# Tokens on the output's partitions for two FFNs and all down and output projections

## The chip, the core and the metric

The kernel runs on one core of a Trainium2 chip. TensorE multiplies matrices out of SBUF into the eight banks of PSUM; VectorE (DVE), ScalarE (ACT) and GpSimd (POOL) work on tiles of 128 partitions; SyncE (SP) issues the DMAs that load the weights. Each engine takes its instructions in the program's order and waits on semaphores for the others. The metric is the time of one execution on the device in microseconds (us), the median of several runs.

## The reference

256 tokens of width 2048 go through a first block twice and through a second block once. A layer of the first block:

```python
h = rmsnorm(x, g_pre_mix[l])
proj = h @ w_in[l]                                     # 2048 x 4608
y_a = conformer_conv(proj[..., :a_end], ...)           # width 512
y_b = dilated_attention(proj[..., a_end:b_end], ...)   # width 1024, 16 heads
y_c = pool_mixer(proj[..., b_end:], ...)               # width 512
y = concatenate([rms_normalize(y_a), rms_normalize(y_b), rms_normalize(y_c)]) * g_mix[l]
x = x + rmsnorm(y @ w_out[l], g_post_mix[l])           # 2048 x 2048
h = rmsnorm(x, g_pre_ffn[l])
f = (silu(h @ w_gate[l]) * (h @ w_up[l])) @ w_down[l]  # 2048 x 5632, twice; 5632 x 2048
x = x + rmsnorm(f, g_post_ffn[l])
```

The second block has the same frame: four branches of width 512 (a gated delta rule, a linear recurrent unit, spatial gating, a short convolution), an output projection of 2048 x 2048, and an FFN with a causal convolution over the tokens behind gate and up. All is float32. The output is compared in float32, which sets how the products are made (below).

## The kernel before

All activations lie with features on the partitions and the 256 tokens along the free axis: a tile of 128 features is [128, 256], the residual x is [128, 16, 256]. Both factors of a product are split into two parts, hi and lo, of TensorE's faster float32 type, and three products (hi hi, hi lo, lo hi) stand for one.

Weights come as a stream (class `Stream`): half chunks of 256 rows by 512 columns, 512 KB each, 1120 in all, in the order of a plan that lists them chunk by chunk. For each, SP issues a load into `st` (4 buffers), ScalarE makes `whi` (L87, 5 buffers) and VectorE `wlo` (L95, 4 buffers). `ahead(i)` emits the splits three half chunks before the products that use them.

`groupA` makes 512 columns of output, features on the output's partitions: for each half chunk four tiles of 128 columns, two row tiles k and three products, 24 matmuls of a stationary weight tile [128, 128] against a moving activation [128, 256] (`mms`, L340 to L342). `dualA` runs the first two groups of a half block together, while the residual is still being updated (`barrier`). Its `step(n)` emits `prep(i)`, which adds f times its norm to x and makes the split operand `hhi`, `hlo` for two row tiles. `groupB` is used for the attention's values and one input of the spatial gating only: the activation [128, 128 tokens] is stationary, the weights [128, 512] move, and 12 matmuls make [128 tokens, 512] in each of two banks (L396 to L398).

The order of the work around the products is made by the program itself. After each half chunk's matmuls `pump()` emits what stands in queues of generators: evacuations of PSUM (`evq`), and background work (`bg`, `hot`), each with an estimate of its VectorE time; the budget is 1450 ns a half chunk, and `yield -1` rests until the next half chunk.

A norm is applied after the products. `R_gen` sums squares on TensorE (`ps_st`), makes the reciprocal root on GpSimd (`rsqrt`, twelve small steps), broadcasts it over the partitions by TensorE (`bcast`, `ps_bc`) and copies it to SBUF as R and Rh; the evacuations multiply by it. An FFN (`ffn`, `ffn_run`) goes over 11 pieces j of 512 hidden columns, gate then up, in three portions, with the down products of a portion behind it; its evacuations make `hid`, the split operand of the down products. f [128, 16, 256] gathers the down or output products. In the last column groups (`last_group`) each part of f gets its squares summed (`sq_add`) and its gain (`gains`); for the very last one `fin_last` takes tile by tile, and `post` (`rsqrt_fast`) makes the norm that `barrier` multiplies by. There are six such ends: three mixers and three FFNs. A mixer's output projection runs by branch: yC, yA (8 half chunks each), then the attention's yb (16), with the attention in the background of the first two.

## Time and profile before

| | before |
|---|---|
| median of 3 runs | 3460.69 us (3459.11 to 3462.64) |
| span of the profiled execution | 3458.9 us |
| TensorE busy, matmul records | 3423.8 us (99%), 27758 |
| VectorE busy | 2180.8 us (63%) |
| ScalarE busy | 1648.5 us (48%) |
| GpSimd busy | 105.0 us (3%) |
| mean granted TensorE clock | 0.993 of full speed |
| read from HBM | 598.84 MB, 175 GB/s over the span |

The profile shows one execution. What lies around its span isn't recorded apart: the runs' median is 1.8 us above it. A matmul's record overlaps the next one's, so the pace of a stream is read from the starts of its records, or from their count in a stretch, not from the length of one. PE is TensorE's matmuls, PEld its weight loads.

### The profile page before, as it was taken

The numbers are of one execution on the slowest core, as the hardware profiler recorded it, in microseconds if no ns is written. First come the engines' busy times: TensorE is split into PE (matmuls) and PEld (weight loads), VectorE is DVE, ScalarE is ACT, GpSimd is POOL, SyncE is SP. The second block draws the span as 40 slices with busy tenths as digits, with TensorE's granted clock in tenths as the row PEclk, the third lists the DMA queues.
The fourth block names the chain that finished last, engine by engine and source line by source line (L and its number), as shares of the span: only waits on it lengthen the run. The fifth ranks groups of instructions, "written<-read, shape, count | busy, mean of one in ns | idle before, by whom it ended". The sixth has DMA issues, their size and how long they took to land.

```text
span 3458.9 us, 66199 instructions
## 1 busy us (share of the span) xinstructions
PE 3423.8 (99%) x27758; PEld 3365.6 (97%) x27758; DVE 2180.8 (63%) x2957; ACT 1648.5 (48%) x2219; POOL 105.0 (3%) x301
## 2 busy tenths in 40 slices
PE   9999999999999999999999999999999999999999
PEld 9989999999999998999999999999999999999998
DVE  6877755455555787775545555578665766466465
ACT  5556544444344555554444334455435554455344
POOL 0000000000000000000000000001110000000000
PEclk9999999999999999999999999999999999999999
DMA  7654566666665565456666666565435665666563
GB/s 234 185 170 142 169 184 183 184 183 184 183 183 182 162 190 164 157 157 186 183 183 181 186 183 183 178 189 165 128 122 190 179 184 184 183 183 182 185 184 130
DMA packets 315436, 609.44 MB, mean 176 GB/s; under 512 B 19168, under 2 KB 24672, under 8 KB 314880
## 3 DMA queue, kind: packets, MB, share of 16 engines
q1 hardware_dynamic: 314224, 599.37, 57.9%
q0 software_dynamic: 912, 5.83, 0.5%
q8 instruction: 217, 3.56, 0.4%
q14 instruction: 83, 0.68, 0.1%
HBM read 598.84 MB, written 6.29 MB: 175 GB/s over the span
## 4 chain that ended last, share of the span: by engine, by line
PE 95%; DVE 2%; POOL 1%; DMA 1%; issue 0%; ACT 0%; SPq 0%; DVEq 0%; POOLq 0%; ACTq 0%
PE ps_mm L340 29%; PE ps_mm L342 29%; PE ps_mm L341 29%; PE ps_st L266 1%; PE ps_mm L352 1%; PE ps_mm L396 1%; PE ps_mm L397 1%; PE ps_mm L398 1%; PE ps_sc L747 0%; PE ps_av L794 0%; DVE wlo L95 0%; PE ps_pt L782 0%; PE ps_bc L314 0%; POOL q L287 0%; POOL q L286 0%
## 5 line engine op out<-in xcount | busy, mean ns | idle before, releaser
L95 DVE TENSOR_TENSOR wlo<-st,whi 128x1024 fp32r<-128x1024 f32 x1120 | 1365.8, 1222 | 923.0 <-PE ps_mm L342 839.4
L87 ACT CAST whi<-st 128x1024 fp32r<-128x1024 f32 x1120 | 1170.5, 1049 | 1250.7 <-PE ps_mm L341 1084.6
L340 PE MATMUL ps_mm<-hhi,whi 128*128 128x256 f32 x5712 | 1621.0, 284 | 0.1
L341 PE MATMUL ps_mm<-hlo,whi 128*128 128x256 f32 x5712 | 1616.6, 283 | 0.1
L342 PE MATMUL ps_mm<-hhi,wlo 128*128 128x256 f32 x5712 | 1616.5, 283 | 0.3 <-DVE wlo L95 0.3
L340 PEld LDWEIGHTS ps_mm<-hhi,whi 128*128 128x128 f32 x5712 | 1096.5, 192 | 1.2 <-issue 0.3
L341 PEld LDWEIGHTS ps_mm<-hlo,whi 128*128 128x128 f32 x5712 | 1096.5, 192 | 0.6 <-DVE hlo L480 0.3
L342 PEld LDWEIGHTS ps_mm<-hhi,wlo 128*128 128x128 f32 x5712 | 1096.4, 192 | 0.6 <-DVE wlo L95 0.5
L340 PE MATMUL ps_mm<-hid,whi 128*128 128x256 f32 x2112 | 597.9, 283 | 0.0
L342 PE MATMUL ps_mm<-hid,wlo 128*128 128x256 f32 x2112 | 597.7, 283 | 0.0
L341 PE MATMUL ps_mm<-hid,whi 128*128 128x256 f32 x2112 | 597.7, 283 | 0.0
L340 PEld LDWEIGHTS ps_mm<-hid,whi 128*128 128x128 f32 x2112 | 405.5, 192 | 0.0
L341 PEld LDWEIGHTS ps_mm<-hid,whi 128*128 128x128 f32 x2112 | 405.5, 192 | 0.0
L342 PEld LDWEIGHTS ps_mm<-hid,wlo 128*128 128x128 f32 x2112 | 405.5, 192 | 0.0
L342 PE MATMUL ps_mm<-y,wlo 128*128 128x256 f32 x448 | 127.4, 284 | 3.8 <-DVE wlo L95 3.8
L340 PE MATMUL ps_mm<-y,whi 128*128 128x256 f32 x448 | 129.9, 290 | 0.0
L341 PE MATMUL ps_mm<-y,whi 128*128 128x256 f32 x448 | 127.3, 284 | 0.0
L340 PEld LDWEIGHTS ps_mm<-y,whi 128*128 128x128 f32 x448 | 86.4, 193 | 4.8 <-issue 2.0
L342 PEld LDWEIGHTS ps_mm<-y,wlo 128*128 128x128 f32 x448 | 86.5, 193 | 4.2 <-DVE wlo L95 4.2
L341 PEld LDWEIGHTS ps_mm<-y,whi 128*128 128x128 f32 x448 | 86.6, 193 | 0.1
L1019 ACT CAST hid<-su 128x512 fp32r<-128x512 f32 x66 | 40.7, 621 | 88.0 <-DVE su L1018 88.0
L474 ACT ACTIVATE hhi<-x,par 128x256 fp32r<-128x256 f32 x84 | 38.2, 501 | 91.9 <-DVE x L468 91.0
(413 smaller groups left out, 2672.7 us busy)
## 6 DMA issues: line engine op xcount, KB each, us to landing
st<-in_w_in_dram SPq DMA_DIRECT2D x232, 512.0 KB
st<-in_w_gate_dram SPq DMA_DIRECT2D x176, 512.0 KB
st<-in_w_up_dram SPq DMA_DIRECT2D x176, 512.0 KB
st<-in_w_down_dram SPq DMA_DIRECT2D x176, 512.0 KB
st<-in_ffn_up_dram SPq DMA_DIRECT2D x176, 512.0 KB
st<-in_w_out_dram SPq DMA_DIRECT2D x96, 512.0 KB
st<-in_ffn_down_dram SPq DMA_DIRECT2D x88, 512.0 KB
xpark<-x POOLq DMA_DIRECT2D x1, 2048.0 KB, 6.9
```

Of the source, the lines that this page charges most:

```text
L87: net.nc.scalar.copy(hi, self.st[h])
L95: net.nc.vector.tensor_tensor(lo, self.st.pop(h), self.hi[h], ALU.subtract)
L266: self.nc.tensor.matmul(ps[:, t:t + 1], a[:, t * P:(t + 1) * P], self.ones[:, 0:1], start=start and i == 0 and t == 0, stop=stop and i == ...
L340: nc.tensor.matmul(o, hi[:, k, w], act[0], start=first and head, stop=False)
L341: nc.tensor.matmul(o, hi[:, k, w], act[1], start=False, stop=False)
L342: nc.tensor.matmul(o, lo[:, k, w], act[0], start=False, stop=last and tail)
L352: mm(ps[j // 2][:, j % 2, :], w[:, k, j * P:(j + 1) * P], acts[k][a], start=n == 0 and k == 0 and j % 2 == 0, stop=False)
L396: nc.tensor.matmul(ps[t], a[0][:, ts], hi[:, k, :], start=h == 0 and k == 0, stop=False)
L397: nc.tensor.matmul(ps[t], a[0][:, ts], lo[:, k, :], start=False, stop=False)
L398: nc.tensor.matmul(ps[t], a[1][:, ts], hi[:, k, :], start=False, stop=h == nh - 1 and k == 1)
L474: nc.scalar.activation(hhi[:, k, :], x[:, k, :], AF.Identity, scale=self.p(g, k))
L1019: nc.scalar.copy(h[:, 0, sl, :], u[:, sl, :])
```

## The change

Gate and up of the two FFNs of the first block, and all down and output projections, are made by `groupB` (with `dualB` for the first pair), so that their outputs have tokens on the partitions. 712 of the 1120 half chunks go over. A norm per token is then a number per partition, and needs no broadcast: R_gen with `rows` makes `rh` (half of the norm, and half of its square) by two more GpSimd steps, and the evacuations use it as a scale; the branches' norms (yA, yC, yb of the first block's mixers) scale their part of f. Four broadcasts for branches, two for yb and two for the FFNs go.

Two things must be turned back to features on the partitions, by `turn`: four TensorE transposes into a bank. u, the product of gate and up, is turned for each j, two turns one half chunk after the group's end, and split from PSUM into `hid`. f is turned column group by column group into a new tile fT, with the gain applied on the way: two turns two half chunks after the group's end (`fin_turn`), and the last two in `post`. The sum of squares comes from ScalarE's accumulator (`fin_half`), not from TensorE. The FFN of the second block keeps its gate and up as they were.

The core of the diff:

```diff
-    def groupB(self, keys, act, evac):
+    def mmsB(self, ps, t, hi, lo, k, act, first, last):
+        mm = self.nc.tensor.matmul
+        ts = slice(t * P, (t + 1) * P)
+        mm(ps[t], act[0][:, ts], hi[:, k, :], start=first, stop=False)
+        mm(ps[t], act[0][:, ts], lo[:, k, :], start=False, stop=False)
+        mm(ps[t], act[1][:, ts], hi[:, k, :], start=False, stop=last)
+    def groupB(self, keys, act, evac=None, now=None):
...
+    def dualB(self, keys0, keys1, act, evac0, evac1, step):
...
+                    if i == 1:
+                        for k in range(2):
+                            a = act(k)
+                            for m, (w, x) in enumerate(((hi, 0), (lo, 0), (hi, 1))):
+                                for t in range(2):
+                                    mm(ps[s][t], a[x][:, t * P:(t + 1) * P], w[:, k, :],
+                                       start=m == 0 and k == 0, stop=False)
+                    else:
+                        for t, k in ([(t, k) for t in range(2) for k in range(2)] if end
+                                     else [(t, k) for k in range(2) for t in range(2)]):
+                            self.mmsB(ps[s], t, hi, lo, k, act(2 * h + k), h == 0 and k == 0, end and k == 1)
...
+    def turn(self, src, base, i):
+        ps = self.bank("ps_tr", (P, 2, T))
+        for k in range(2):
+            c = base + (2 * i + k) * P
+            for t in range(2):
+                self.nc.tensor.transpose(ps[:, k, t * P:(t + 1) * P], src[:, t, c:c + P], self.ident)
+        return ps
...
         yield 500
+        if rows:
+            self.rh = self.sm.tile([P, 4], F32, tag="rh", name="rh", bufs=2)
+            self.nc.gpsimd.tensor_scalar(self.rh[:, 0:2], self.r_tok, 0.5, None, ALU.mult)
+            self.nc.gpsimd.tensor_tensor(self.rh[:, 2:4], self.rh[:, 0:2], self.r_tok, ALU.mult)
+            return
...
+        def scaled(r):
+            def add(t, o, ps):
+                V.scalar_tensor_tensor(o, ps, getattr(self, r)[:, t:t + 1], o, ALU.mult, ALU.add)
+            return add
...
     def last_group(self, keys, act, cg, add, gen=None):
-        nc = self.nc
         if cg < 3:
             def ev(ps):
+                for t in range(2):
+                    self.fin_half(t, cg, ps[t], add)
+                    yield 800
+                yield -1
                 for i in range(2):
-                    k = 4 * cg + 2 * i
-                    add(self.f[:, k:k + 2, :], ps[i])
-                    self.sq_add(self.f[:, k:k + 2, :], nc.vector)
-                    yield 1200
-                    self.gains(k)
-            self.groupA(keys, act, self.after(gen, ev) if gen else ev)
+                    self.fin_turn(cg, i)
+                    yield 0
+            self.groupB(keys, act, self.after(gen, ev) if gen else ev)
...
+    def fin_half(self, t, cg, ps, add):
+        o = self.fcol(cg)[:, t, :]
+        add(t, o, ps)
+        junk = self.tmp("sq").rearrange("p a b -> p (a b)")
+        self.nc.scalar.activation(junk, o, AF.Square, accum_out=self.ss[:, t, cg:cg + 1])
+    def fin_turn(self, cg, i):
+        ps = self.turn(self.f, 512 * cg, i)
+        for j in range(2):
+            k = 4 * cg + 2 * i + j
+            self.nc.scalar.activation(self.fT[:, k, :], ps[:, j, :], AF.Identity, scale=self.p(self.fin_g, k))
...
         def ev_gate(j):
             def ev(ps):
...
+                for t in range(2):
+                    nc.scalar.activation(th[t], ps[t], AF.Tanh, scale=self.rh[:, t:t + 1])
+                yield 0
+                for t in range(2):
+                    V.scalar_tensor_tensor(sub[j][:, 0, t, :], th[t], 1.0, ps[t], ALU.add, ALU.mult)
                     yield 660
...
         def ev_up(j):
             def ev(ps):
-                s, u = sub[j][:, 0:4, :], sub[j][:, 4:8, :]
+                s, u = sub[j][:, 0], sub[j][:, 1]
+                for t in range(2):
+                    V.scalar_tensor_tensor(u[:, t, :], ps[t], self.rh[:, 2 + t:3 + t], s[:, t, :], ALU.mult, ALU.mult)
+                    yield 660
+                yield -1
+                h = self.ug.tile([P, 2, 4, T], F32R, tag="ug", name="hid")
                 for i in range(2):
-                    V.tensor_tensor(u[:, 2 * i:2 * i + 2, :], ps[i], self.b2(self.Rh), ALU.mult)
-                    yield 600
-                yield from self.hid_gen(hid, j, u, s)
+                    sl = slice(2 * i, 2 * i + 2)
+                    pt = self.turn(u, 0, i)
+                    nc.scalar.copy(h[:, 0, sl, :], pt)
+                    V.tensor_tensor(h[:, 1, sl, :], pt, h[:, 0, sl, :], ALU.subtract)
+                    yield 660
+                hid[j] = h
```

How the order of the instructions moves, at three places. First TensorE in the first FFN, behind its opening pair of groups. Before, the norm's broadcast stands two half chunks behind the pair:

```order
L340 MATMUL ps_mm<-hhi,whi 128x256
L341 MATMUL ps_mm<-hlo,whi 128x256
L342 MATMUL ps_mm<-hhi,wlo 128x256
L314 MATMUL ps_bc<-ident,r_pre 128x128 x2
L340 MATMUL ps_mm<-hhi,whi 128x256
```

After, the first turned tile stands there, three half chunks behind the pair (su is the tile that holds u):

```order
L369 MATMUL ps_mm<-wlo,hhi 128x512
L370 MATMUL ps_mm<-whi,hlo 128x512
L429 MATMUL ps_tr<-ident,su 128x128 [waits DVE_49,PE_49]
L429 MATMUL ps_tr<-ident,su 128x128 [waits DVE_49]
L429 MATMUL ps_tr<-ident,su 128x128 x2
L429 MATMUL ps_tr<-ident,su 128x128 [waits PE_49]
L429 MATMUL ps_tr<-ident,su 128x128 x3
L368 MATMUL ps_mm<-whi,hhi 128x512 [waits Activation_49]
```

The products of one weight tile are half as many and twice as wide, and eight transposes wait for VectorE's u. Second, VectorE at the same opening (v to r_pre are the start of the norm, th the tanh of the gate). Before:

```order
L284 TENSOR_SCALAR r_pre<-ti 128x2 [waits DVE_49]
L95 TENSOR_TENSOR wlo<-st,whi 128x1024 [waits DMAHW0_49,Activation_49]
L95 TENSOR_TENSOR wlo<-st,whi 128x1024 [waits DMAHW1_49,PE_49,Activation_49]
L992 TENSOR_TENSOR su<-ps_mm,R 128x512 [waits Activation_49]
L992 TENSOR_TENSOR su<-ps_mm,R 128x512
L997 SCALAR_TENSOR_TENSOR su<-th,su 128x512 [waits Activation_49]
L95 TENSOR_TENSOR wlo<-st,whi 128x1024 [waits DMAHW2_49,PE_49]
```

After:

```order
L284 TENSOR_SCALAR r_pre<-ti 128x2 [waits DVE_49]
L1046 SCALAR_TENSOR_TENSOR su<-th,ps_mm 128x512 [waits Activation_49] x2
L95 TENSOR_TENSOR wlo<-st,whi 128x1024 [waits DMAHW0_49]
L1054 SCALAR_TENSOR_TENSOR su<-ps_mm,rh,su 128x512 [waits DVE_49,Pool_49]
L1054 SCALAR_TENSOR_TENSOR su<-ps_mm,rh,su 128x512 [waits DVE_49]
L95 TENSOR_TENSOR wlo<-st,whi 128x1024 [waits DMAHW1_49,PE_49,Activation_49]
```

The two weight splits that stood between the norm's start and its first use now stand behind it. Third, TensorE at the end of a mixer. Before, three pieces of the sums (sql are squares from ScalarE) lie between the last product and the broadcast of r_post:

```order
L342 MATMUL ps_mm<-yb_2576,wlo 128x256
L266 MATMUL ps_st<-ones,sql 128x1 [waits Activation_49]
L266 MATMUL ps_st<-ones,sql 128x1 x3
L266 MATMUL ps_st<-ones,sql 128x1 [waits Activation_49]
L266 MATMUL ps_st<-ones,sql 128x1
L266 MATMUL ps_st<-ones,sql 128x1 [waits Activation_49]
L266 MATMUL ps_st<-ones,sql 128x1
L314 MATMUL ps_bc<-ident,r_post 128x128 [waits DVE_49,PE_49]
```

After:

```order
L370 MATMUL ps_mm<-whi,yb_2560 128x512
L429 MATMUL ps_tr<-ident,f 128x128 [waits DVE_49] x2
L429 MATMUL ps_tr<-ident,f 128x128 x2
L429 MATMUL ps_tr<-ident,f 128x128 [waits PE_49]
L429 MATMUL ps_tr<-ident,f 128x128 x3
L301 MATMUL ps_bc<-ident,r_post 128x128 [waits DVE_49] x2
```

The sums have left TensorE, and the last eight transposes of f stand in their place.

## Rows read from the trace of the kernel before

**Rows 1.** The page, part 1: busy time, share of span and instructions.
```profile
PE 3423.8 (99%) x27758; PEld 3365.6 (97%) x27758; DVE 2180.8 (63%) x2957; ACT 1648.5 (48%) x2219; POOL 105.0 (3%) x301
```

**Rows 2.** By stretch (us): length, busy per engine (instructions), PEclk, DMA share, GB/s.
```profile
0.00:60.00 60.00, 53.28 (x421) 52.90 (x422) 37.23 (x54) 33.40 (x45) 2.42 (x10) 1.00 0.80 256
...
590.00:1118.00 528.00, 528.00 (x4402) 528.00 (x4402) 275.39 (x268) 219.88 (x236) 0.00 (x0) 1.00 0.62 183
```

**Rows 3.** Timeline, VectorE, first FFN: start, length, operation, [idle before <-releaser].
```profile
602.55 1.22 DVE L95 TENSOR_TENSOR wlo<-st,whi 128x1024 fp32r<-128x1024 f32 x1 [1.66 <-PE ps_mm L342]
```

**Rows 4.** Timeline, TensorE, the attention's values of the first layer.
```profile
82.00 0.39 PE L396 MATMUL ps_mm<-whi,hhi 128*128 128x512 f32 x1
...
99.00 0.39 PE L396 MATMUL ps_mm<-whi,hhi 128*128 128x512 f32 x1
...
101.23 0.58 PE L396 MATMUL ps_mm<-whi,hhi 128*128 128x512 f32 x1
101.64 0.39 PE L397 MATMUL ps_mm<-wlo,hhi 128*128 128x512 f32 x1
```

**Rows 5.** Chain that ended last, in time: start, us, engine, tile, records.
```profile
99.85 1.73 PE ps_pool L678 x8
...
240.33 0.87 PE ps_pt L782 x8
...
246.78 1.02 PE ps_pt L782 x8
...
349.36 0.79 PE ps_st L266 x8
...
357.21 4.55 PE ps_mm L352 x24
...
411.70 0.70 PE ps_bc L314 x4
```

**Rows 6.** Timeline, all engines, behind the first FFN's opening pair.
```profile
404.89 0.95 PE L266 MATMUL ps_st<-ones,sqacc 128*128 128x1 f32 x8
...
406.53 1.11 POOL L286 TENSOR_TENSOR q<-r_pre 128x2 f32<-128x2 f32 x1 [91.76 <-DVE r_pre L284]
...
407.71 0.20 POOL L287 TENSOR_TENSOR q<-q,h 128x2 f32<-128x2 f32 x1
...
411.43 0.20 POOL L289 TENSOR_TENSOR r_pre<-q,r_pre 128x2 f32<-128x2 f32 x1
...
412.83 1.29 DVE L992 TENSOR_TENSOR su<-ps_mm,R 128x512 f32<-128x512 f32 x2 [2.69 <-ACT R L320]
```

**Rows 7.** TensorE's waits over the span: total us, times, longest.
```profile
PE ps_bc L314 <- POOL r_y L289: 2.7, 2, 1.4
```

**Rows 8.** Timeline, the end of the first mixer.
```profile
350.69 0.28 PE L342 MATMUL ps_mm<-yb,wlo 128*128 128x256 f32 x1
...
350.13 0.63 ACT L966 ACTIVATE sql<-f 128x512 f32<-128x512 f32 x1 [1.54 <-DVE f L924]
...
353.31 0.26 ACT L298 ACTIVATE v<-ps_st,eps 128x2 f32<-128x2 f32 x1 [0.89 <-DVE h L296]
...
353.67 0.17 DVE L299 RECIPROCAL r_post<-v 128x2 f32<-128x2 f32 x1 [0.19 <-ACT v L298]
...
354.57 1.19 PE L314 MATMUL ps_bc<-ident,r_post 128*128 128x128 f32 x4 [1.49 <-DVE r_post L302]
```

**Rows 9.** Groups by form: busy us, mean ns of one, idle before.
```profile
L782 PE MATMUL ps_pt<-ident,ring 128*128 128x128 f32 x128 | 17.4, 279 | 0.0
...
L762 ACT ACTIVATION_READ_ACCUMULATOR ring<-ring,am 128x1 f32 x64 | 11.9, 187 | 0.0
```

**Rows 10.** Timeline, VectorE, the opening of the first FFN (prep of pairs 3 and 7).
```profile
368.17 0.68 DVE L467 TENSOR_TENSOR f<-f,ps_bc 128x512 f32<-128x512 f32 x1
...
390.81 0.68 DVE L467 TENSOR_TENSOR f<-f,ps_bc 128x512 f32<-128x512 f32 x1
```

**Rows 11.** By stretch, TensorE alone, after the first mixer's end: length, busy, PEclk, DMA.
```profile
358.00:359.00 1.00, 1.00 (x6) 0.50 0.00 0
```

More of the change, by code (lines that the diff above doesn't have):

```diff
@@ L377, in groupA @@
                     self.mms(ps, j, hi, lo, k, act(2 * h + k), h == 0 and k == 0, h == nh - 1 and k == 1)
-                if now and h == nh - 1 and j:
-                    now(j, ps[j - 1])
-            if evac and h == nh - 1:
+            if h == nh - 1:
                 self.later(evac(ps))
@@ L402, in groupB, with dualA @@
         return self.gid
-    def dualA(self, keys0, keys1, act, evac0=None, evac1=None, step=None, now=None):
+    def dualB(self, keys0, keys1, act, evac0, evac1, step):
+        mm = self.nc.tensor.matmul
+        gids, ps = [], []
+        for _ in range(2):
+            ps.append(self.new_ps((P, 512)))
+            gids.append(self.gid)
+        n = len(keys0)
+        i = 0
+        for c in range(n):
+            for s, keys in ((0, keys0), (1, keys1)):
+                for b in range(2):
+                    step(i)
+                    i += 1
+                    hi, lo = self.W.get(keys[c], b)
+                    h = 2 * c + b
+                    end = h == 2 * n - 1
+                    if i == 1:
[9 more added lines that the diff above has]
+                            self.mmsB(ps[s], t, hi, lo, k, act(2 * h + k), h == 0 and k == 0, end and k == 1)
+                    if end:
+                        self.evq.append((gids[s], (evac0, evac1)[s](ps[s])))
+                    self.pump()
+        self.lag = 1
+        return gids
+    def turn(self, src, base, i):
[5 more added lines that the diff above has]
+        return ps
+    def dualA(self, keys0, keys1, act, evac0, evac1, step):
         gids = []
@@ L415, in dualA @@
                 for b in range(2):
-                    if step:
-                        step(i)
+                    step(i)
                     i += 1
@@ L449, in hk, with barrier @@
         return self.hhi[:, k, :], self.hlo[:, k, :]
-    def barrier(self, g, fg=None, Rps=None):
+    def barrier(self, g, fg=None, Rps=None, rows=False):
         nc = self.nc
@@ L599, in ln_gen, with y_gen @@
         yield from self.y_gen(z, self.g_half, 0.5, "yA")
-    def y_gen(self, z, g, sc, name):
+    def y_gen(self, z, g, sc, name, norm=False):
         nc = self.nc
@@ new lines, in post @@
+    def post(self):
+        V = self.nc.vector
+        ss, sb = self.ss, self.sb
+        r = self.sm.tile([P, 2], F32, tag="r_post", name="r_post", bufs=2)
+        q = self.sm.tile([P, 2], F32, tag="q_post", name="q_post", bufs=2)
+        for i in range(2):
+            self.fin_turn(3, i)
+        for t in range(2):
+            rt, qt, h = r[:, t:t + 1], q[:, t:t + 1], sb[:, t, 3:4]
+            V.scalar_tensor_tensor(h, ss[:, t, 3:4], -0.5 / D, sb[:, t, 1:2], ALU.mult, ALU.add)
+            V.reciprocal(rt, sb[:, t, 2:3])
+            V.scalar_tensor_tensor(qt, rt, h, rt, ALU.mult, ALU.mult)
+            V.scalar_tensor_tensor(rt, qt, 1.5, rt, ALU.add, ALU.mult)
@@ L1025, in hid_gen, with ffn_run @@
             yield 600
-    def ffn_run(self, nm, gpost, step, ev_gate, ev_up, hid):
+    def ffn_run(self, nm, gpost, step, ev_gate, ev_up, hid, rows=False):
         nc = self.nc
@@ L1035, in gu @@
             if j == 0:
-                gids[j] = self.dualA(kg, ku, self.hk, ev_gate(0), ev_up(0), step)[1]
+                gids[j] = (self.dualB if rows else self.dualA)(kg, ku, self.hk, ev_gate(0), ev_up(0), step)[1]
             else:
-                self.groupA(kg, self.hk, ev_gate(j))
-                gids[j] = self.groupA(ku, self.hk, ev_up(j))
+                group = self.groupB if rows else self.groupA
+                group(kg, self.hk, ev_gate(j))
+                gids[j] = group(ku, self.hk, ev_up(j))
         def down(js, first, last):
             if first:
-                self.f = self.act.tile([P, KD, T], F32, tag="big", name="f", bufs=3)
+                self.f_alloc()
             if last:
                 self.fin_start(gpost)
-            f = self.f
             def act(k):
@@ L1313, in y2_gen @@
         self.nc.vector.tensor_scalar(gt, self.p("grp", 4 * i, 4), sc, None, ALU.mult)
-        yield from self.y_gen(z, lambda k: gt[:, k:k + 1], sc, name)
+        yield from self.y_gen(z, lambda k: gt[:, k:k + 1], sc, name, norm=True)
     def gdn_evacs(self):
```

167 lines of the change are left out of this document (62 added, 105 removed).

## The prediction

> **What bounds the kernel now.** The page comes first: TensorE is busy for 99% of the span, every other engine for far less [rows 1]. A busy share doesn't say at what pace it works, so the next view is the table by stretch: in the body of the first FFN 4402 products start in 528.00 us at the full granted clock of 1.00 (the 2.4 GHz level), 119.95 ns each, while VectorE and ScalarE are busy for about half of it [rows 2]. One half chunk of weights (256 rows by 512 columns) is 24 such products, 2.879 us. The line of VectorE there shows who waits for whom: it splits a half chunk in 1.22 us and then sits for 1.66 us until TensorE is done with an older one [rows 3]. So weights are not what is late; the number of products times their pitch is. What a change saves or adds on TensorE counts in full, what it saves on VectorE or ScalarE counts nothing, unless it makes TensorE wait.
>
> **The wide products (the gain).** The kernel has the new form already, in the attention's values: 75 products of 512 columns go from 82.00 to 99.00 us, 226.7 ns each [rows 4]. Two narrow ones do the same work in 239.9. The change turns 17088 narrow products into 8544 wide ones: 712 half chunks of the 1120 (the instruction counts of both programs), each 12 x 226.7 = 2.720 instead of 2.879 us. 712 x 0.159 = **-113.1 us**, all on the path. The shapes, types and pools of the values' products are those of the new ones, so I leave this term no width of its own while weights arrive in time.
>
> A page of the Trainium skill speaks against this term: "TensorE: Matmul & The Clock Gate", section "Back-to-back issue gap", gives the isolated gap as N / 2.4 GHz plus about 2.5 ns. By that rule a wide product would save 2.5 ns, 8544 of them 21 us, and the sum below would be +15 us, a time of 3475 us. The trace has 13.3 ns above 106.7 and 13.3 ns above 213.3 (both worked out from the pitches above and the 2.4 GHz level), so the rule doesn't describe these streams, and I follow the rows.
>
> **The transposes (the price).** 368 come in: 176 turn the two FFNs' hidden tiles, 192 turn f at the six ends. They stand in visits of eight: 22 for hidden tiles, 18 for f behind products, 6 at the very ends. The attention's transposes of the same size take 1.02 us for eight, and 0.87 in the shortest case [rows 5]. Going back from such float32 work costs a little more: the first wide product after it is followed at 0.41 us and not at 0.227 [rows 4]. So a visit is 1.02 + 0.18 = 1.20 us, and 40 visits on the path are **+48.0 us**. The bounds are 0.87 each (34.8) and the dearest like row, eight float32 product records in 1.73 plus 0.18 (76.4); I take the middle one, since it is the same instruction with the same identity. The six visits at the ends lie where TensorE waits for a norm anyway (below).
>
> **Who would make a visit wait.** TensorE works in order, so all later products stand behind a transpose whose tile isn't ready. A hidden tile is emitted one half chunk after its group's last product, so VectorE has 2.72 us. It needs 0.65 for each half of the tokens (1.29 for two like operations [rows 6]), and the first half is complete 1.4 us before the second; the last is ready some 0.8 us after the last product, even if one weight split of 1.22 stands in front it is 2.0. For f there are two half chunks. I price these waits at nothing; the cover is a margin of 0.7 to 1.9 us. VectorE itself gets less to do: six operations for a hidden tile instead of ten, ScalarE four as before.
>
> **What goes from TensorE.** Eight broadcasts of a norm (two before the FFNs, four for the branches' y, two for the attention's) at 0.70 each [rows 5], 5.6 us, and the waits in front of the two for yC, 2.7 us [rows 7]: **-8.3 us**. The first part of the sum of squares in each end's last group, 0.79 each [rows 5], six times: **-4.7 us**. The VectorE passes that used these broadcasts go too, beside other work: nothing.
>
> **The ends.** Between the last product and the broadcast of the norm the first mixer takes 3.88 us [rows 8]: two short additions, a square, the rest of the sums on TensorE, ScalarE's root, four small VectorE steps. The new chain is one product of 0.39 [rows 4], one addition of 0.65 [rows 6], a square of 0.63, a root of 0.26 and three steps of 0.17 [rows 8], and the read of the square's accumulator, 0.19 [rows 9]; 2.6 in all, and some 0.4 for five handovers (estimated from the gaps between these rows): 3.0 to 3.1. The mixers gain 0.8, the ends with one addition 0.4: 2 x 0.8 + 3 x 0.4 = **-2.8 us**. At the last end the broadcast stands behind copies of x on TensorE as before; nothing. The eight transposes need only f, which is ready after the addition, and are through when the root is; what is late next is the same norm.
>
> **The opening of the two FFNs (a new wait).** Before, R was broadcast two half chunks after its sums, so VectorE kept splitting weights meanwhile. Now the first tanh and everything behind it on ScalarE, and two VectorE operations with the next weight split behind them, stand in line for GpSimd's result. The chain in the trace: sums from 404.89 us, GpSimd from 406.53 to 411.63 [rows 6]. Two of its twelve steps take 1.1 us, the others 0.20, and the slow ones start while VectorE splits weights; now VectorE stands still, so I take 0.28 a step (with gaps): ready at 1.6 + 3.4 + 0.6 for two more steps = 5.6 us after the sums began. Then two tanh (0.63 each, as the square in [rows 8], the second beside VectorE), two gate operations, a split of 1.22 and two up operations: some 10.1 us. TensorE has three half chunks until its first transposes, 0.8 + 3 x 2.72 = 9.0. So it waits 1.2 us in each FFN, **+2.5 us**; with the GpSimd steps as slow as in the trace it would be 3 each, 6; 0 if the order is kinder. Also, in the first 12 half chunks VectorE needs 5.66 us for two (four periods between the two rows of [rows 10]), TensorE 5.76 before and 5.44 after. TensorE will lean on VectorE there. Its lead of three half chunks covers most of that; the second FFN has more small work beside it: **+1.5 us** (0 to 3.5).
>
> **The sum.** -113.1 + 48.0 - 8.3 - 4.7 - 2.8 + 2.5 + 1.5 = -76.9 us. The profiled execution spans 3458.9 us; the median of the runs is 3460.69, 1.8 more, which I keep. **3384 us.**
>
> **The rivals.**
> (a) The clock stays up over the ends. After an end the granted clock is 0.50 (the 1.2 GHz level) [rows 11], and 24 products take 4.55 us [rows 5] instead of 2.88. If transposes in the gap prevent the drop, five ends give 1.7 each: 8.5 us, **3375 us**. For it: TensorE's gap gets shorter. Against: the sums on TensorE stood in the same gap and the clock fell all the same.
> (b) The transposes make TensorE wait. If VectorE or ScalarE lags by one split more than I think, each of the 40 visits stands for about 1 us: +40, **3424 us**. For it: TensorE is in order, and the tile passes one or two engines shortly before. Against: the idle time of VectorE [rows 3]. Break-even only from 1.9 us a visit.
> (c) A transpose costs its latency and doesn't overlap. Its place would be the switch between products and transposes: the rows for eight give 1.02, but one record lasts 279 ns [rows 9], and eight of these end to end would be 2.23 us, with the 0.18 2.4 a visit, 96 for the forty where the sum has 48.0: **3432 us**. Against: the same rows. The Trainium skill, "TensorE: Matmul & The Clock Gate", section "Part 4: PE-mode transpose", prices one at about 275 ns in a kernel; 320 on the path would be 88 us in place of 48.0.
> (d) Slower: the weights can't come faster. The loads move 183 GB/s through all of the FFN's body [rows 2], so flat that it could be their limit. Then a half chunk of 512 KB takes 2.865 us whatever TensorE does, the wide products save 10 us, and the rest adds: -10 + 48.0 - 8.3 - 4.7 - 2.8 + 2.5 = +25, **3485 us**. It decides from 2.83 us a half chunk on, 185 GB/s. Against: the first 60 us run at 256 GB/s [rows 2], and splits wait for TensorE, not for loads [rows 3].
>
> **How the numbers follow.** Forecast 0.70, (a) 0.08, (b) 0.11, (c) 0.03, (d) 0.05; 0.01 for the rule's 3475; 0.02 for a weaker form of (d) that leaves no difference. The forecast's own bounds reach from 3364 (cheap visits, some of (a)) to 3414 (dear visits and openings); with (a) inside, that is 0.78, and the edge of (b) makes it 8 in 10. Faster (by over 0.2%, about what a measurement of this kernel can tell from no change): 0.92; within 0.2%: 0.02; slower: 0.06.
>
> **What would show it.** Wide products in the FFN's body at 227 ns a start, and a half chunk of weights every 2.72 us; if 2.88, (d). Eight transposes in about 1.0 us with the next product right behind; if there is idle time in front of them with VectorE as its releaser, (b). An idle stretch of a microsecond or so before the first transposes of each FFN. The broadcast of the norm about 3.1 us after the last product. The clock after each end at half. What would make the prediction wrong is above all the price of a visit, since 40 of them stand on the path: each 0.25 us is 10 us.

## The result, and the profile after

The changed kernel takes 3361.54 us (median of 4 runs, 3361.41 to 3361.97) beside 3460.28 for the kernel before: a ratio of 0.9715, 95% interval 0.9701 to 0.9729. Faster was right, but the time lies 2.5 us below the range given (3364 to 3414), and 22.5 below the forecast. The profiled execution spans 3359.5 us, 99.4 less than before.

The page's part 1 of the changed kernel shows 30% fewer matmul records (transposes among them), and TensorE busy for 99% as before [rows 1]:

```profile
PE 3326.9 (99%) x19406; PEld 2924.7 (87%) x19406; DVE 2102.6 (63%) x2847; ACT 1652.6 (49%) x2261; POOL 106.4 (3%) x305
```

By stretch, 43.5 us of the first FFN's body between two visits of transposes, and TensorE's timeline in the same body (start, length; 51 rows stand between the two shown):

```profile
443.30:486.80 43.50, 43.50 (x195) 36.05 (x193) 23.46 (x22) 18.95 (x20) 0.00 (x0) 1.00 0.63 192
```

```profile
500.05 0.39 PE L368 MATMUL ps_mm<-whi,hhi 128*128 128x512 f32 x1
...
511.83 0.39 PE L369 MATMUL ps_mm<-wlo,hhi 128*128 128x512 f32 x1
```

52 steps in 11.78 us are 226.5 ns each, the pitch of the attention's values [rows 4]; loads now run at 192 GB/s where [rows 2] had 183. To see where the rest went, I cut both programs into the same stretches, by the start of the first product of each half chunk in TensorE's timeline. The last column is the forecast's own sum for that stretch.

| stretch | before | after | difference | forecast |
|---|---|---|---|---|
| two FFN bodies, 243 half chunks each | 2 x 699.84 | 2 x 672.64 | -54.4 | -46.0 |
| two FFN openings: the pairs, 16 each | 48.50, 50.24 | 47.26, 49.10 | -2.4 | -3.6 |
| behind the pairs, 4 each | 2 x 12.27 | 12.58, 12.57 | +0.6 | +2.2 |
| five ends: last half chunk to the next block's first product | 49.47 | 36.79 | -12.7 | -7.6 |
| the last end | 21.52 | 18.76 | -2.8 | -0.9 |
| two mixers behind their opening pairs | 290.51, 288.48 | 283.38, 282.51 | -13.1 | -9.5 |
| second block: output projection | 91.28 | 89.45 | -1.8 | -1.3 |
| second block: FFN behind its pair | 712.11 | 700.94 | -11.2 | -10.2 |
| all others (unchanged work) | | | -1.7 | 0 |
| sum (of unrounded parts) | | | -99.4 | -76.9 |

The first row settles the price of a visit: 243 x 12 x 0.2267 = 661.1 us of products leave 11.6 for 13 visits, 0.89 each, not 1.20. The chain of waits of the changed kernel has them one by one (start, us, tile, records; two of them here), and TensorE's timeline shows the way in and out of one:

```profile
487.08 0.87 PE ps_tr L429 x8
531.50 0.87 PE ps_tr L429 x8
```

```profile
442.26 0.40 PE L370 MATMUL ps_mm<-whi,hlo 128*128 128x512 f32 x1
442.50 1.04 PE L429 MATMUL ps_tr<-ident,su 128*128 128x128 f32 x8
443.29 0.48 PE L368 MATMUL ps_mm<-whi,hhi 128*128 128x512 f32 x1
443.60 0.40 PE L369 MATMUL ps_mm<-wlo,hhi 128*128 128x512 f32 x1
```

From 487.08 to 531.50 are 16 half chunks of 2.72 and one visit: 44.42 - 43.52 = 0.90. There is no idle time in front of the transposes, and the first product behind them is followed at 0.31 us, 0.08 more than usual, not 0.18 more.

The end of the first mixer, in the timeline of all engines (to be held against [rows 8]):

```profile
342.39 0.39 PE L370 MATMUL ps_mm<-whi,yb 128*128 128x512 f32 x1
...
344.44 0.39 PE L301 MATMUL ps_bc<-ident,r_post 128*128 128x128 f32 x2
...
345.35 0.49 PE L301 MATMUL ps_bc<-ident,r_post 128*128 128x128 f32 x2 [0.52 <-DVE r_post L1029]
345.88 0.42 DVE L495 TENSOR_TENSOR fT<-fT,ps_bc 128x256 f32<-128x256 f32 x1 [0.58 <-PE ps_bc L301]
...
347.29 1.19 PE L411 MATMUL ps_mm<-whi,hhi 128*128 128x512 f32 x2 [1.45 <-DVE hhi L499]
```

The broadcast's last part starts 2.96 us after the last product (before 3.88), and VectorE has it 0.53 us later (before 1.22): half of it went out 0.9 us earlier, and the rest finds TensorE at the full clock. The windows of both kernels say so (length, busy per engine, PEclk). First the changed kernel, around this broadcast, then over the ends of the first mixer and the first FFN:

```profile
345.00:346.00 1.00, 0.49 (x2) 0.30 (x2) 0.39 (x3) 1.00 (x4) 0.00 (x0) 1.00 0.00 0
...
341.00:361.00 20.00, 17.30 (x68) 13.69 (x67) 16.49 (x38) 10.16 (x22) 0.00 (x0) 0.83 0.34 98
1081.00:1098.00 17.00, 14.35 (x98) 13.41 (x97) 14.03 (x34) 8.69 (x19) 0.00 (x0) 0.90 0.24 71
```

As the clock has two levels (half is 0.50), a mean of 0.83 over 20 us is 6.8 us at half, 0.90 over 17 is 3.4. In the kernel before the same broadcast stood at half clock, and so did the copies of x at the very end:

```profile
3443.00:3446.00 3.00, 3.00 (x5) 1.45 (x6) 1.01 (x6) 2.63 (x7) 0.00 (x0) 0.50 0.00 0
354.57:355.70 1.13, 1.13 (x4) 0.89 (x4) 0.00 (x0) 1.13 (x4) 0.00 (x0) 0.50 0.00 0
```

In the changed kernel the stretch of those copies has the full clock:

```profile
3345.00:3350.00 5.00, 5.00 (x18) 2.49 (x17) 3.08 (x8) 2.36 (x8) 0.00 (x0) 1.00 0.00 0
```

The opening of the first FFN, timeline of all engines:

```profile
398.76 0.23 POOL L533 TENSOR_SCALAR rh<-r_pre 128x2 f32<-128x2 f32 x1
...
399.03 1.27 ACT L1043 ACTIVATE th<-ps_mm,rh 128x512 f32<-128x512 f32 x2 [5.41 <-POOL rh L533]
...
402.08 1.40 DVE L1054 SCALAR_TENSOR_TENSOR su<-ps_mm,rh,su 128x512 f32<-128x512 f32 x2
...
402.63 0.39 PE L370 MATMUL ps_mm<-whi,hlo 128*128 128x512 f32 x1
402.98 0.30 PE L429 MATMUL ps_tr<-ident,su 128*128 128x128 f32 x1
403.54 0.98 PE L429 MATMUL ps_tr<-ident,su 128*128 128x128 f32 x7 [0.27 <-DVE su L1054]
```

The wait that was foreseen is there, by the chain that was foreseen, but shorter: the first tanh starts 5.3 us after the sums on TensorE (393.74), where 5.6 was summed. From the last product (402.63) to the next stream's first (404.28) are 1.65 us, in the body 1.03: 0.6 of waiting for u.

### The profile page after: what moved, and what is told of

It reads as the page before. It is cut to its first block, busy times and chain, and to the rows that moved or that the text cites. A ratio compares the mean times of both kernels' runs of the same rounds, so it can differ in the third digit from the quotient of the medians.

```text
span 3359.5 us, 49619 instructions
## 1 busy us (share of the span) xinstructions
PE 3326.9 (99%) x19406; PEld 2924.7 (87%) x19406; DVE 2102.6 (63%) x2847; ACT 1652.6 (49%) x2261; POOL 106.4 (3%) x305
## 4 chain that ended last, share of the span: by engine, by line
PE 95%; DVE 2%; ACT 1%; DMA 1%; POOL 1%; issue 0%; SPq 0%; DVEq 0%; POOLq 0%
PE ps_mm L368 19%; PE ps_mm L369 19%; PE ps_mm L370 19%; PE ps_mm L324 10%; PE ps_mm L325 10%; PE ps_mm L326 10%; PE ps_tr L429 1%; DVE wlo L95 1%; PE ps_sc L784 1%; PE ps_av L831 0%; PE ps_pt L819 0%; PE ps_mm L336 0%; PE ps_st L266 0%; PE ps_P L1550 0%; PE ps_T L1563 0%
## 5 line engine op out<-in xcount | busy, mean ns | idle before, releaser
L324 PE MATMUL ps_mm<-hhi,whi 128*128 128x256 f32 x2912 | 828.5, 285 | 0.7 <-ACT hhi L502 0.7
L325 PE MATMUL ps_mm<-hlo,whi 128*128 128x256 f32 x2912 | 824.5, 283 | 0.1
L326 PE MATMUL ps_mm<-hhi,wlo 128*128 128x256 f32 x2912 | 824.3, 283 | 0.0
L368 PE MATMUL ps_mm<-whi,hhi 128*128 128x512 f32 x1560 | 611.0, 392 | 0.3 <-ACT hhi L502 0.2
L369 PE MATMUL ps_mm<-wlo,hhi 128*128 128x512 f32 x1560 | 607.6, 389 | 1.4 <-DVE wlo L95 1.4
L370 PE MATMUL ps_mm<-whi,hlo 128*128 128x512 f32 x1560 | 607.7, 390 | 0.0
L324 PEld LDWEIGHTS ps_mm<-hhi,whi 128*128 128x128 f32 x2912 | 559.0, 192 | 1.9 <-ACT hhi L502 0.9
L325 PEld LDWEIGHTS ps_mm<-hlo,whi 128*128 128x128 f32 x2912 | 559.0, 192 | 0.7 <-DVE hlo L508 0.3
L326 PEld LDWEIGHTS ps_mm<-hhi,wlo 128*128 128x128 f32 x2912 | 558.8, 192 | 0.2 <-DVE wlo L95 0.2
L368 PE MATMUL ps_mm<-whi,hid 128*128 128x512 f32 x1056 | 412.2, 390 | 0.0
L370 PE MATMUL ps_mm<-whi,hid 128*128 128x512 f32 x1056 | 411.1, 389 | 0.0
```

What stands on the lines that cost most here:

```text
L324: nc.tensor.matmul(o, hi[:, k, w], act[0], start=first and head, stop=False)
L325: nc.tensor.matmul(o, hi[:, k, w], act[1], start=False, stop=False)
L326: nc.tensor.matmul(o, lo[:, k, w], act[0], start=False, stop=last and tail)
L368: mm(ps[t], act[0][:, ts], hi[:, k, :], start=first, stop=False)
L369: mm(ps[t], act[0][:, ts], lo[:, k, :], start=False, stop=False)
L370: mm(ps[t], act[1][:, ts], hi[:, k, :], start=False, stop=last)
```

## The experiments

The theory that the traces suggest (A): a visit costs 0.89, the transposes' own pitch and hardly anything for the switch; that is 40 x 0.31 = 12.4 of the 22.5 us. The rest lies at the ends, by a broadcast that goes out in halves and a clock that falls later. The rival (B): a visit does cost 1.20, and something else paid for it. Totals of different sets differ (the kernel before took 3457.1, 3458.1 and 3458.0 us in the three sets below, 3460.28 above), so effects of a few us are read by stretch against the changed kernel's profile (span 3359.5).

**e1: every visit behind products done twice.**

```diff
+        for _ in range(n):
             for k in range(2):
                 c = base + (2 * i + k) * P
                 for t in range(2):
                     self.nc.tensor.transpose(ps[:, k, t * P:(t + 1) * P], src[:, t, c:c + P], self.ident)
```

n is 2 for hidden tiles and for the first three column groups of f.

> Each of the 40 visits of transposes that stand behind products does its eight transposes twice into the same bank (the second time writes the same values), 320 more. The trace after the change shows the visits 44.42 us apart over 16 half chunks of 2.72, that is 0.90 a visit. Theory A (a visit is eight transposes at their pitch of about 0.107 us and next to nothing for the switch): 320 x 0.107 = +34 us over the changed kernel, 3396 us. Theory B (the forecast's price, 1.20 a visit or 0.15 a transpose, with a gain elsewhere that hid it): +48, 3410. Theory C (a transpose costs the 273 ns of its record): +87, 3449.

Measured: 3394.82 us, span 3392.9, +33.4. The chain of waits of this run:

```profile
444.30 1.75 PE ps_tr L430 x16
```

Eight more transposes cost 0.88 here, and the body grew by 11.35 us for 13 visits, 0.87 each: 0.109 us a transpose. Theory A; B as priced here and C are out. A dear switch, which doing the transposes twice would not show, is left to e2.

**e2: no transposes of hidden tiles.**

```diff
-                    pt = self.turn(u, 0, i)
+                    pt = u.rearrange("p t (k c) -> p (t k) c", k=2)[:, sl, :]
```

> The transposes of the hidden tiles are left out: hid is split from u as it lies in SBUF, so the down products get the wrong layout. 176 transposes in 22 visits go; ScalarE's copy and VectorE's subtraction stay. Theory A: 22 x 0.89 = 19.6 us, and with them the two short waits for u at the FFNs' openings (about 0.8 each): -21 over the changed kernel, 3340 us. Theory B: 22 x 1.20 + 1.6 = -28, 3334 us.

Measured: 3338.86 us, span 3337.5, -22.0. Both bodies are 9.00 us shorter for ten visits, 0.90 each with the way in and back; the stretch behind each opening pair is 1.55 shorter, a visit and 0.66 of waiting. That is A within a microsecond, and as a whole visit is worth no more than 0.90, no dear switch stands beside the transposes. Even with no visit a half chunk takes 2.72 us, so the weights keep up.

**e3: gate and up narrow again.**

```diff
-        s.ffn(l, s.barrier(f"g_pre_ffn.{l}", fg, R, rows=True))
+        s.ffn(l, s.barrier(f"g_pre_ffn.{l}", fg, R))
...
-                for t in range(2):
-                    nc.scalar.activation(th[t], ps[t], AF.Tanh, scale=self.rh[:, t:t + 1])
+                for i in range(2):
+                    V.tensor_tensor(s[:, 2 * i:2 * i + 2, :], ps[i], self.b2(self.R), ALU.mult)
+                    nc.scalar.activation(t[i], s[:, 2 * i:2 * i + 2, :], AF.Tanh, scale=0.5)
...
```

> One part undone: gate and up of the two FFNs are made as before, features on the output's partitions, norm broadcast; down and output projections stay wide. 352 half chunks go back to 24 narrow products. Theory A: +352 x 0.159 = +55.9, -22 x 0.89 = -19.6 for the visits, +1.4 for two broadcasts, -1.5 for the opening waits, some -2 for the second opening: +34 over the changed kernel, 3396 us. Theory B (visits at 1.20): +27, 3389 us.

Measured: 3394.99 us, span 3394.2, +34.7: A's +34 and not B's +27. Each body is 16.03 us longer: 160 half chunks x 0.159 = 25.4, less ten visits, so (25.4 - 16.0) / 10 = 0.94 a visit. By the edited stretches alone it is +33.8. So gate and up of two FFNs are some 34 us of the gain, down and output projections and the ends the other 65.

**e4: no rest before the turn.**

```diff
-                yield -1
                 h = self.ug.tile([P, 2, 4, T], F32R, tag="ug", name="hid")
```

> The rest of one half chunk before the turn of a hidden tile is taken out: its transposes stand right behind the group's last product and wait for VectorE's u. Theory A (the rest covers a wait): as at the ends, the second half of u is ready some 1.1 to 1.2 us after the last product's start, so TensorE waits about 0.9 a visit, 22 x 0.9 = +20 us, 3382 us; twice that if a weight split of 1.22 stands in front of u on VectorE. Rival (the rest is not needed, other work or the pipeline covers it): within 2 us of the changed kernel.

Measured: 3387.43 us, span 3384.8, +25.3. Timeline of this run at a visit in the first FFN, and its line in the table of TensorE's waits:

```profile
441.04 0.75 DVE L1054 SCALAR_TENSOR_TENSOR su<-ps_mm,rh,su 128x512 f32<-128x512 f32 x1 [0.30 <-PE ps_mm L370]
...
442.21 0.27 PE L429 MATMUL ps_tr<-ident,su 128*128 128x128 f32 x1
...
442.41 0.75 DVE L1054 SCALAR_TENSOR_TENSOR su<-ps_mm,rh,su 128x512 f32<-128x512 f32 x1 [0.62 <-PE ps_mm L370]
443.22 0.55 PE L429 MATMUL ps_tr<-ident,su 128*128 128x128 f32 x3 [0.73 <-DVE su L1054]
```

```profile
PE ps_tr L429 <- DVE su L1054: 20.6, 24, 2.7
```

Each turn in the body costs 1.03 us more (+10.27 for ten); the two openings cost 4.37 and 2.73 more (in the first the clock fell too, for 3.4 us). The second half of u starts when the group's last product is done, and TensorE stands for its 0.75. So the rest of one half chunk is what makes rival (b) of the prediction harmless.

**e5: one broadcast at the ends, not two halves.**

```diff
-            V.scalar_tensor_tensor(rt, qt, 1.5, rt, ALU.add, ALU.mult)
+        V.scalar_tensor_tensor(r, q, 1.5, r, ALU.add, ALU.mult)
```

> One part of the ends undone: the last small VectorE step of the norm makes both token halves at once, so that all four broadcast products stand behind it, as in the kernel before; in the changed kernel two of the four are done one microsecond earlier. Theory A (of the 0.7 us that an end is shorter behind the broadcast, the split gives 0.2, as the broadcast of the third mixer before took 0.72 us at the full clock and now 0.53; the rest is the clock, which fell before the broadcast in four of the five ends before): +0.2 an end, 6 ends, +1.1 us over the changed kernel. Rival (the split gives all of it, or without it the clock falls earlier again): +0.7 an end, +4 us.

Measured: 3361.38 us, span 3358.5; each of the five ends 0.22 to 0.23 longer (7.62 for 7.39 us at the first), VectorE starting 0.75 us after the broadcast does and not 0.53:

```profile
344.10 0.71 PE L301 MATMUL ps_bc<-ident,r_post 128*128 128x128 f32 x4 [0.74 <-DVE r_post L1029]
344.85 0.42 DVE L495 TENSOR_TENSOR fT<-fT,ps_bc 128x256 f32<-128x256 f32 x1 [0.80 <-PE ps_bc L301]
```

As A says; the total hides it, since in this execution the clock did not fall behind the first mixer (the pair is 1.44 shorter), and that differs between executions of the same code. In all five ends the clock is still full when the broadcast starts.

**e6: TensorE kept busy in the ends.**

```diff
+        self.warm(6)
         for i in range(2):
             self.fin_turn(3, i)
...
             self.nc.tensor.matmul(ps[:, t * P:(t + 1) * P], r[:, t:t + 1].to_broadcast([P, P]), self.ident)
+            self.warm((4, 12)[t])
```

warm(n) makes n transposes of the identity into a bank of their own.

> TensorE gets work in the five ends that lead on to a next block: 6 more transposes of the identity before the last turns, 4 and 12 behind the two halves of the broadcast, all in its idle time. Theory A (a drop of 3.4 us behind an end costs nothing, since VectorE's preparation of the operand sets the pace there: 48.50 us for the second mixer's first pairs with a drop and without; only the 6.8 us at the first FFN costs, 47.26 against 45.80): no drops, and 0 to -1.5 us against the changed kernel. Rival (the clock is worth half of each drop, rival (a) of the forecast): 16 us of half clock over busy TensorE go, -5 to -8 us. Second rival (22 more transposes delay the broadcast or the first product): slower by up to 5.

Measured: 3359.84 us, span 3357.1. By stretch, the first of the five ends in this run (the others read 1.00 as well):

```profile
340.00:360.00 20.00, 18.95 (x97) 14.95 (x96) 16.46 (x38) 10.13 (x22) 0.00 (x0) 1.00 0.32 99
```

The clock is 1.00 over all five ends, no end is longer, and behind them only the first FFN's pair is shorter, by 1.44 us: theory A (another 1.0 of the span's -2.4 lies in the first mixer, ahead of the edit). The second mixer's pair takes 48.50 us with 3.4 us of half clock (the changed kernel) and 48.50 with none (here).

**e7: the first hidden tile turned one half chunk later.**

```diff
-                yield -1
+                for _ in range(2 if j == 0 else 1):
+                    yield -1
```

> The first hidden tile of each FFN is turned one half chunk later. Theory A (TensorE waits 0.66 us there for u, which is late behind GpSimd's norm): -0.7 in each of two openings, -1.3 us against the changed kernel. Rival (VectorE's lateness comes back as a wait for weight splits right behind): 0.

Measured: 3360.90 us (3358.68 to 3363.07), span 3361.0. The stretch behind each opening pair is 0.75 us shorter, as A says, and the rest of each FFN's body is 0.10 longer. The span hides it: the program's first pair, before anything that was edited, took 2.80 us longer in this execution.

**e8: the second block's small operations moved.**

```diff
     def small_gen(self):
         nc = self.nc
+        for _ in range(24):
+            yield -1
```

> The parameters that the second block makes on VectorE (some 22 small operations, 4.4 us) start 24 half chunks later, not in the opening of the second FFN. Theory A (they make TensorE wait there: half chunks of 4.85, 2.93, 2.95, 2.94, 2.97 and 2.91 us where 2.72 stands in the first FFN): the opening takes 45.8 to 46.1 instead of 49.1 us, -3 us. Rival (VectorE's steady work of 5.66 us for two half chunks sets that pace anyway): 0.

Measured: 3358.11 us, span 3356.2; the second FFN's pair takes 45.82 us, 3.28 less. VectorE's timeline in the changed kernel, from the first to the last of 24 small operations and to what stood behind them (fT and wlo):

```profile
1431.42 0.18 DVE L1285 TENSOR_SCALAR hw<-par 128x48 f32<-128x48 f32 x1
...
1435.65 0.16 DVE L1294 TENSOR_SCALAR lsp<-sp 128x4 f32<-128x4 f32 x1
1435.72 0.68 DVE L495 TENSOR_TENSOR fT<-fT,ps_bc 128x512 f32<-128x512 f32 x1
...
1438.50 2.35 DVE L95 TENSOR_TENSOR wlo<-st,whi 128x1024 fp32r<-128x1024 f32 x2
```

and in this run the two splits at the same place:

```profile
1432.84 2.36 DVE L95 TENSOR_TENSOR wlo<-st,whi 128x1024 fp32r<-128x1024 f32 x2
```

The 4.4 us were in front of the next operand and the weight splits. Without them VectorE's steady work lets the pair run at TensorE's pace, so the lean on VectorE that the prediction feared came from these alone.

**e9: e6, e7 and e8 together.**

> The changed kernel with three edits together: TensorE kept busy in the five ends, the first hidden tile of each FFN turned one half chunk later, the second block's small operations moved out of the second FFN's opening. Theory A (each worked in a place of its own, so they add): -1.5 (first FFN's opening pair 47.26 to 45.8) -1.5 (two openings, 0.75 each) -3.3 (second FFN's opening pair 49.10 to 45.8) = -6 us against the changed kernel, a span of 3353. Rival (the openings hand a wait on to the next, above all the later turn and the moved operations, both on VectorE): -3 to -4.

Measured: 3354.88 us, ratio to the kernel before 0.9703 (0.9689 to 0.9716), span 3353.6, -5.9; the first FFN's pair -1.47, the second's -3.28, the stretches behind them -0.75 each. The gains add as A says. This is the fastest version that computes the whole. By the ratios to the kernel before (0.9703 beside 0.9715, with intervals that overlap) it is some 4 us below the changed kernel, by the spans and the stretches 6.

**e10: no transposes in the ends' idle time.**

```diff
-        for i in range(2):
-            self.fin_turn(3, i)
+        for k in range(4):
+            c = 512 * 3 + k * P
+            self.nc.scalar.activation(self.fT[:, 12 + k, :].rearrange("p (a b) -> p (a b)", a=2), self.f[:, :, c:c + P],
+                                      AF.Identity, scale=self.p(self.fin_g, 12 + k))
```

> The last eight transposes of f at each of the six ends are left out (ScalarE copies those columns from f as it lies, so the output is wrong). They lie in TensorE's idle time, so by themselves they cost nothing. Theory A (they are what keeps the clock up until the broadcast): without them the clock falls before the broadcast in most ends, as in the kernel before, the broadcast takes 1.0 us or more to VectorE's first use in place of 0.53, ends are 5.3 us or more from the last product to the next block's first in place of 4.84 to 4.91, and more drops of 6.8 us follow: +3 to +7 us. Rival (the shorter gap does it, the transposes don't matter): gaps of 4.84 to 4.91 as with them, and the time within 2 us.

Measured: 3361.25 us, span 3359.8. Timeline at the end of the first FFN, and by stretch before and behind its broadcast:

```profile
1080.28 0.39 PE L370 MATMUL ps_mm<-whi,hid 128*128 128x512 f32 x1
...
1083.17 0.49 PE L301 MATMUL ps_bc<-ident,r_post 128*128 128x128 f32 x2 [0.54 <-DVE r_post L1031]
1083.70 0.42 DVE L495 TENSOR_TENSOR fT<-fT,ps_bc 128x256 f32<-128x256 f32 x1 [0.58 <-PE ps_bc L301]
1085.12 0.55 PE L336 MATMUL ps_mm<-hhi,whi 128*128 128x256 f32 x1 [1.45 <-DVE hhi L499]
```

```profile
1080.00:1083.00 3.00, 1.12 (x5) 0.50 (x4) 2.15 (x10) 2.56 (x8) 0.00 (x0) 1.00 0.56 175
1084.00:1085.00 1.00, 0.00 (x0) 0.00 (x0) 0.90 (x3) 0.07 (x1) 0.00 (x0) 0.50 0.00 0
```

Theory A fell here: the ends stay at 4.84 to 4.91 us and the broadcast at 0.53, with TensorE idle for most of the gap. The transposes of f are not, by themselves, what holds the clock until the broadcast.

**e11: the kernel before, TensorE kept busy in its ends.**

```diff
         r = self.rsqrt_fast(self.pst[:, 0:2], 1.0 / D, 2, "r_post")
         self.gains(KD)
+        self.warm(8)
...
+        ps = self.bcast(r)
+        self.warm(12)
```

> The kernel before, with 8 transposes of the identity in front of the norm's broadcast and 12 behind it at the five ends, in TensorE's idle time; nothing of the change is in it. Theory A (half of the unforeseen gain at the ends is the clock): in the four ends where it fell before the broadcast that takes 0.72 in place of 1.15 to 1.23 us, -0.5 each, and the drops of 6.8 us and more behind the ends cost 1 us or so each: -4 to -6 us against the kernel before, and so much less of a gain for the change where both have the clock. Rival (the clock costs nothing there, VectorE's preparation of the operand sets the pace): within 1.5 us of the kernel before.

Measured: 3455.11 us beside 3458.0, ratio 0.9991 (0.9982 to 1.0000). This one does not decide. At the end of the first mixer the broadcast did get the full clock, but the clock fell behind it all the same, and twelve transposes at half clock took 2.77 us and held up the first product (at the ends of both FFNs and of the third mixer even the broadcast stood at half clock, 1.09 to 1.23 us from its start to VectorE):

```profile
351.80 0.76 PE L315 MATMUL ps_bc<-ident,r_post 128*128 128x128 f32 x4 [0.56 <-DVE r_post L303]
352.35 2.77 PE L322 MATMUL ps_w<-ident 128*128 128x128 f32 x12
...
354.77 0.56 PE L365 MATMUL ps_mm<-hhi,whi 128*128 128x256 f32 x1
```

The pairs behind the five ends are 0.4 to 1.7 us shorter (4.4 in sum), three of the ends 0.3 to 1.8 longer (2.8 in sum). What the clock alone was worth in the kernel before stays open.

## Why the prediction was off, point by point

**The wide products: right.** 226.5 ns a start in the body, 2.72 us a half chunk; the table's first row holds only with the full -113.1. Rival (d) didn't come: loads went from 183 to 192 GB/s. The rule of the Trainium skill ("TensorE: Matmul & The Clock Gate", section "Back-to-back issue gap"), by which the time would have been 3475 us, is not what this chip did: the streams take some 13.3 ns more than their columns at 2.4 GHz, at 256 columns and at 512.

**The price of a visit: the step that failed.** "I take the middle one, since it is the same instruction with the same identity": the instruction was the same, but what stands in front of it and behind it was not. The kernel before had other cases; its TensorE timeline in the attention:

```profile
240.04 0.28 PE L342 MATMUL ps_mm<-y,wlo 128*128 128x256 f32 x1
240.17 1.03 PE L782 MATMUL ps_pt<-ident,ring 128*128 128x128 f32 x8
241.13 0.92 PE L747 MATMUL ps_sc<-k,q 64*128 64x256 f32 x6
...
245.70 1.08 PE L794 MATMUL ps_av<-ring,v 128*64 128x256 f32 x8
246.72 1.09 PE L782 MATMUL ps_pt<-ident,ring 128*128 128x128 f32 x8
247.74 0.49 PE L747 MATMUL ps_sc<-k,q 64*128 64x256 f32 x2
...
280.56 1.09 PE L782 MATMUL ps_pt<-ident,ring 128*128 128x128 f32 x8
281.40 0.36 PE L340 MATMUL ps_mm<-y,whi 128*128 128x256 f32 x1
281.61 0.28 PE L341 MATMUL ps_mm<-y,whi 128*128 128x256 f32 x1
```

Behind the products of the weights the eight are 0.96 us from first start to the next stream's, behind ps_av's float32 products 1.02; and the chain gives 0.87 to the first and 1.02 to the second [rows 5]. What stands behind counts for more: ps_sc starts 0.20 us after the last of the eight in both, but the weight products at 281.40 only 0.03 after it, so there the eight take 0.84 with ps_av in front. The visits to be priced stand between weight products, 0.79 us from start to start in the changed kernel; by the chain's measure the row to take was 0.87, the lower bound. The addition of 0.18 for going back came from eight larger float32 products; here it is 0.08, and it was 0.08 at 281.40 too (0.20 to the next start, where 0.12 is usual). At 0.89 the 40 visits cost 35.6 us and not 48.0, which is 12.4 of the 22.5 us. The Trainium skill's figure of some 275 ns for a transpose in bf16 ("TensorE: Matmul & The Clock Gate", section "Part 4: PE-mode transpose") is near the length of one float32 record here, 273 ns, but in a row they cost 109 ns each.

**The waits in front of a visit: right at nothing,** with the rest of a half chunk as the reason (e4: 1.03 us a visit without it). Rivals (b) and (c) are out.

**The ends: undersized by 5.1 us.** Forecast -7.6 with the last half chunk and the sums, measured -12.7. Four parts, from the two traces: the broadcast after the last product comes 4.0 us earlier in sum, not 2.8 (1.2; one of the ends before, the second mixer's, had its sums at half clock); between the broadcast and VectorE 2.9 us go where I had counted nothing: 1.1 by the halves (e5, 0.22 an end), 1.8 by the clock, which before stood at half in four of these five broadcasts; and the last half chunk gains 1.0 more, since the sums also cost going in and back. The sum of the new chain, "3.0 to 3.1", was good to 0.1 to 0.2 (2.90 to 2.97), but I let the chain stop at the broadcast's start and carried its length over.

**The last end: undersized by 1.8.** The copies of x, which the forecast left as they were, ran at half clock before and run at the full clock now: the first four take 1.7 us and not 3.4.

**The clock: partly rival (a).** "The clock after each end at half" holds at four of the five ends, but it falls later, and at three of them for 3.4 us where it was 6.8 or more. It is worth less than (a) said, though: at 1.7 us an end I priced each drop as if TensorE set the pace behind it. The preparation of the operand on VectorE and ScalarE does: 3.4 us at half cost nothing at the second mixer, where TensorE at the full clock waits 0.7 us for hhi instead (e6), and at most 0.25 at the first FFN (e4, e8); 6.8 us cost 0.8 to 1.5 (by the pairs behind the ends in the changed kernel, e5, e8 and e10). Why it falls later is not settled. The transposes don't do it by themselves (e10), nor does the half of the broadcast that goes out at 2.0 us (e5); no run left out both. A shorter gap remains as the likely cause, argued and not shown.

**The openings: right in kind, too dear.** The wait was 0.7 an FFN (e2, e7) and not 1.2; the lean on VectorE was absent in the first FFN, and in the second it was 24 small operations that happen to stand there (e8). Of the table's two rows, the pairs are 1.2 us worse than forecast, and what stands behind them is 1.6 better (0.6 of it the visits' price, 1.0 the wait).

**What is left.** Visits 12.4, ends 5.1, last end 1.8, opening waits 1.0: 20.3 of 22.5. The other 2.2 are several small ones: the pairs 1.2 worse, the mixers 1.7 better than with visits at 0.89, and 1.7 in unchanged work, half of it the second block's FFN pair (49.48 to 48.53) with less half clock behind the end. The mixers' 1.7 stands in one half chunk, the first of the first mixer's output projection: 8.81 us before, with 3.4 us of half clock in it, and 6.86 after. It took 6.84 and 6.25 in the second mixer and 5.7 to 6.9 in the other runs, so this part is luck of the profiled execution and not the change.

**The range** ended at 3364, which was visits at 0.87 (13 us) and most of rival (a) (7 us) together. It had no room for ends that come out shorter than summed; another 3 us for that would have held the time.

## What to carry to other kernels

A price for a moved instruction is taken from the row that has the same neighbours, in front and behind, not only the same form: here the same eight transposes took 0.79 to 1.02 us by what stood around them, and the trace of the kernel before had three of the cases. A chain that ends in a product must be followed to the first instruction that uses it, with the clock that the stretch will have, and an unproved gain belongs in the range like an unproved cost. Turning tiles by eight TensorE transposes paid off (0.89 us for eight, against 16 x 0.159 = 2.5 us that the wide form saves on a hidden tile's gate and up), as long as one half chunk of other products lies between the last product of the tile and its turn.

## What the runs showed of the hardware

- Float32 transposes of 128 by 128 in a row cost 109 ns each (e1), with records of 273 ns that overlap; the change between them and the stream of wide products costs almost nothing: 0.02 us of the 0.89. Between other neighbours it costs more: from start to next start eight take 0.79 us between weight products, 0.84 with ps_av in front, 0.96 with ps_sc behind, 1.02 with both.
- The granted clock behind an end differs between executions of the same code: behind the first mixer it was half for 6.8 us (the changed kernel, e7), 3.4 us (e4, e8) or not at all (e2). With 22 small transposes filling the 4.9 us gaps it was 1.00 at all five ends (e6 and again e9), while in the kernel before 20 of them at other places of a longer gap did not hold it (e11).
- A drop of the clock is not a loss by itself: where TensorE waits for its operand anyway, 3.4 us at half left the second mixer's pair at 48.50 us.
